# A decoder layer on one core: seven block products for four of 22 pairs of the down product, weight sums made in place, x's scaling and the projections' evictions ahead in VectorE's order

## The chip, the cores and the metric

The kernel runs on one core of a Trainium2 chip. The metric is the device time of one execution, in microseconds (us), as the median of several runs. TensorE (PE in the profile) does the matrix products, VectorE (DVE) and ScalarE (ACT) the elementwise work, GpSimd (POOL) a few fills, and SyncE (SP) issues nearly all DMAs.

## The reference, cut to what matters

```python
def swiglu(x, w_gate, w_up, w_down):
    return (jax.nn.silu(x @ w_gate) * (x @ w_up)) @ w_down
...
h = h + 0.5 * swiglu(rms_norm(h, ffn1_norm), w_gate1, w_up1, w_down1)
p = rms_norm(h, mix_norm) @ w_in
y = concatenate([rwkv7_time_mix(p[..., :3360]), rglru_mix(p[..., 3360:])])
h = h + y @ w_out
h = h + 0.5 * swiglu(rms_norm(h, ffn2_norm), w_gate2, w_up2, w_down2)
return rms_norm(h, final_norm)
```

There are 256 tokens, a model width of 2048, a hidden width of 5632 (44 tiles of 128), and everything is float32.

## The kernel before, in words

**Products.** A float32 product is made of three float32r products: every operand is split into hi (a copy rounded to float32r, made by ScalarE) and lo (the operand less hi, made by VectorE), and `three` (L133 to L138) issues hi times hi, hi times lo and lo times hi into one PSUM bank of 512 columns. So each block of 128 rows of the contraction, 128 tokens and 512 columns costs three matmuls.

**Weights.** They come from memory in pieces of 1 MB (two tiles of 128 rows, 1024 columns) into the buffers `wst` of a pool with three buffers. ScalarE writes `whi` and VectorE writes `wlo`, in pieces of 128x1024, also with three buffers each. `weights` (L49 to L90) does this for the first chunk of gate and up, for the mixer's projections, for the output projection and for all of the down products; the splits are on L81 and L82. `pairs` (L103 to L130) does it for the other chunks of gate and up, by `split` (L93 to L101), whose splits are on L99 and L100.

**Block products.** In those chunks two tiles of 128 rows, the two halves of the tokens and two blocks of 512 columns form a 2 by 2 by 2 product of blocks. A pair of kind "n" takes the plain eight block products (24 matmuls). A pair of kind "S" takes seven (21 matmuls): it needs four sums of weight blocks, made by VectorE into a second buffer of the `wst` pool (L125, L127 and L128), four sums of x's blocks (`sums`), and four more banks (`aux`) for the products that several results share; `shared` adds those together. An S pair splits seven blocks of 128x512 where an n pair splits four. The plans are "nSnSnSnn" for gate and for up, so three of eight pairs are S. A chunk is 1024 columns of the hidden width; the first chunk is 512 wide and takes the plain path.

**Order.** The framework writes out one fixed order for each engine before the run: it walks the program by an estimate of the times and at each point takes, among the instructions that are ready, the one with the smallest number; the number is the place in the program less an offset where `high_priority(offset=...)` stands. The DMAs and splits of weights have an offset of 4000; all else around the change has none.

**x's scaling.** The first chunk multiplies x before the row's norm is known. After each two tiles of the first up product, `normalised` (L274 to L292) scales that pair of x in place, splits it again (ScalarE L281, VectorE L279, L280 and L282), and for the three S pairs makes x's sums (L286 to L289, L291 and L292). The next chunk's gate product needs them.

**Down.** `ffn` ends with the down product: 44 tiles of the hidden values against 1024 columns at a time (in the second feed-forward block 1024, 512 and 512), by `weights` and `rows_times` (L174, L175 and L177). The last chunk's hidden values are transposed (`hidden_T`, 16 transposes on L263, splits on L270 and L271) after 12 of the 44 tiles of the first piece. Each piece ends with four additions of half of a bank to h (L371).

**Mixer.** Each projection (L186 to L188) fills one or two of three banks; its result leaves them on VectorE, multiplied with the row norms (L571 in `shifted`, L895 in `lru`, L935 in `lru_gate`).

Of the kernel before, what the change touches and what calls it, by code (L numbers as in the profile page):

```python
# [18 lines left out]
EPS = 1e-6  # L19


class Core:
# [80 lines left out]
    def pairs(self, mat, c0, plan):  # L103


        nc = self.nc
        ns = plan.count("S")
        ids = {"S": iter(range(ns)), "n": iter(range(ns, self.NK // 2))}
# [31 lines left out]
    def rows_times_pairs(self, mat, c0, plan, own, aux, xhi, xlo, sums, hooks):  # L140
# [3 lines left out]
        for at, (kind, p, w) in enumerate(self.pairs(mat, c0, plan)):  # L144
            first, last = at == 0, at == len(plan) - 1
            if kind == "n":
                for kk in range(2):
                    for t in range(2):
                        x = [v[:, 2 * p + kk, t * P : (t + 1) * P] for v in (xhi, xlo)]
                        for n in range(2):  # L150
                            self.three(own[2 * t + n], x, w[kk][n], first and kk == 0, last and kk == 1)
            else:
                x = lambda k, t: tuple(v[:, 2 * p + k, t * P : (t + 1) * P] for v in (xhi, xlo))
                sm = lambda n: tuple(sums[:, p, h, n * P : (n + 1) * P] for h in range(2))
# [91 lines left out]
def ffn(core, xhi, xlo, rstd, wg, wu, wd, after_first, after_down, fpool, down, rest, back, head=None):  # L246
# [11 lines left out]
    def hidden_T(c0, w, hid):  # L258
        for j in range(0, w // P, 2):
# [13 lines left out]
            )  # L273

    def normalised(p):
# [7 lines left out]
        if p < NSUM:  # L283
            blk = lambda k, t: tmp[:, k, t * P : (t + 1) * P]
            raw = scrap[:, 1, 512:].rearrange("p (n s) -> p n s", n=4)
            nc.vector.tensor_tensor(raw[:, 0], blk(0, 1), blk(1, 1), ALU.add)  # L286
            nc.vector.tensor_tensor(raw[:, 1], raw[:, 0], blk(0, 0), ALU.subtract)
            nc.vector.tensor_tensor(raw[:, 2], blk(0, 0), blk(0, 1), ALU.subtract)
            nc.vector.tensor_tensor(raw[:, 3], blk(1, 0), raw[:, 1], ALU.subtract)  # L289
            flat = raw.rearrange("p n s -> p (n s)")  # L290
            nc.scalar.copy(sums[:, p, 0, :], flat)  # L291
            nc.vector.tensor_tensor(sums[:, p, 1, :], flat, sums[:, p, 0, :].bitcast(F32), ALU.subtract)  # L292
# [12 lines left out]

    pending = []
    ks = list(range(NK))
    for c0, w in chunks:
        if c0:
# [5 lines left out]
            core.rows_times_pairs(wg, c0, GATE_PLAN, own, aux, xhi, xlo, sums, hooks)  # L315
# [5 lines left out]
            core.rows_times_pairs(wu, c0, UP_PLAN, own, aux, xhi, xlo, sums,  # L321
# [4 lines left out]
            pending = [lambda c0=c0, w=w, hid=hid: hidden_T(c0, w, hid)]  # L326
# [15 lines left out]
        for i, (k, hi, lo) in enumerate(core.weights([(wu, c0, w)], ks)):  # L342
# [3 lines left out]
            if i % 2:  # L346
                normalised(i // 2)
# [8 lines left out]
    back()  # L356
    bank0 = 0
    for piece, (c0, w) in enumerate(down):
        nb = w // 512
        db = [[core.bank((bank0 + t * nb + n) % 8) for n in range(nb)] for t in range(NT)]  # L360
        bank0 += NT * nb
        for i, (k, hi, lo) in enumerate(core.weights([(wd, c0, w)], list(range(NF)))):
            core.rows_times(db, hT_hi, hT_lo, k, hi, lo, w, i == 0, i == NF - 1)
            if i == NF // 4:
                for f in pending:
                    f()
                pending = []
# [13 lines left out]
class Mix:  # L381
# [182 lines left out]
    def shifted(self, bks, ntile, mu0, dst):  # L564

        nc = self.nc
        for b, bk in enumerate(bks):
# [321 lines left out]
    def lru(self, hf, bks):  # L889
# [4 lines left out]
        for b, bk in enumerate(bks):  # L894
            nc.vector.tensor_tensor(  # L895
                XB[:, 2 * b : 2 * b + 2, 3:259], bk.rearrange("p (a s) -> p a s", a=2), self.core.rb[:, None, :].to_broadcast([P, 2, 256]), ALU.mult
            )
# [33 lines left out]
    def lru_gate(self, hf, bks, H):  # L931
        nc = self.nc
        G = self.slot("gate")[:, :1024]
        for b, bk in enumerate(bks):
            nc.vector.tensor_tensor(  # L935
                G[:, b * 512 : b * 512 + 512].rearrange("p (a s) -> p a s", a=2),
                bk.rearrange("p (a s) -> p a s", a=2), self.core.rb[:, None, :].to_broadcast([P, 2, 256]), ALU.mult,
            )
# [106 lines left out]
HIDDEN_AT = 6  # L1045


@with_exitstack
def kernel(ctx: ExitStack, tc: tile.TileContext, dram: dict, out: bass.AP):
# [33 lines left out]
    def xt_pool(stack, name, **kw):  # L1083
        pool = stack.enter_context(tc.tile_pool(name=name, bufs=1, **kw))
        return [pool.tile([P, NK, S], F32R, name=name + n) for n in ("hi", "lo")]

    with ExitStack() as front:
        xa = xt_pool(front, "xa")
        with ExitStack() as st:
# [22 lines left out]
            def rest():  # L1112
                return hpool.tile([P, NSUM, 2, 512], F32R, name="xsums1", tag="h")
# [7 lines left out]
            def park(hf):  # L1121
                norm_half(1, hf, *xa)
# [5 lines left out]
                first_norm, park, fpool, [(0, HD), (HD, HD)], rest, back, head={q: partial(norm_quarter, q + 1) for q in range(3)})  # L1128
# [11 lines left out]
        xb = xt_pool(ctx, "xb", **right)  # L1140
# [6 lines left out]
    with ExitStack() as st:  # L1147
# [17 lines left out]
        def rest2():  # L1165
            t = h2.tile([P, core.NT * D + 504], F32R, name="xsums2", tag="h")
            return t[:, : NSUM * 1024].rearrange("p (n h f) -> p n h f", n=NSUM, h=2)
# [3 lines left out]
            lambda: norm_rows(2, 7), closing, fpool, down, rest2, back2)  # L1171
# [37 lines left out]
```

## Time and profile before

| what | value |
|---|---|
| runs | 1953.81, 1951.44, 1953.48 us; median 1953.48 us |
| the profiled execution's own time | 1948.99 us |
| its span | 1947.3 us |
| mean granted clock of TensorE | 0.994 |
| HBM | 184 GB/s over the span |

The profile is of one execution on the chip. A matmul's listed duration overlaps with that of the next, so the pace of a stream is read from the starts. VectorE's instructions overlap a little too. In brackets behind an instruction stands how long its engine idled before it, and what ended that.

### The profile page before, as it was taken

What the parts mean: (1) busy time and instruction counts of PE and PEld (TensorE: products, weight loads), DVE (VectorE), ACT (ScalarE), POOL (GpSimd) and SP (SyncE); (2) the same over time, 40 slices, a digit from 0 to 9 for tenths busy, and PEclk for the clock granted to TensorE, in tenths of its full rate; (3) what the DMA queues carried; (4) which work ended last, traced back from release to release, by engine and by line L of the source; (5) the groups of instructions that cost most, each with busy time, mean ns of one, the idle gap of its engine ahead of it and who ended that gap; (6) DMA issues with size and microseconds to landing.
All of it is one profiled execution on the core that took longest, in us unless ns stands there. A gap on an engine that the chain in (4) does not pass through costs nothing.

```text
span 1947.3 us, 25669 instructions
## 1 busy us (share of the span) xinstructions
PE 1907.3 (98%) x10233; PEld 1589.7 (82%) x10233; DVE 1440.3 (74%) x1822; ACT 985.8 (51%) x1189; POOL 9.9 (1%) x53
## 2 busy tenths in 40 slices
PE   8899999999999999999999999999999999999997
PEld 6678877878888889998899878778888888788886
DVE  5989898888645446876696775899898989844553
ACT  6465555555444335544454555565556555543443
POOL 0000000000000001000000000000000000000000
PEclk9999999999999999999999999999999999999999
DMA  6356555565755556545243456555555655766553
GB/s 238 129 198 214 173 194 195 178 212 190 264 186 204 194 195 207 177 127 163 77 144 115 131 195 215 173 194 182 199 197 198 211 183 184 257 211 193 195 194 129
DMA packets 130032, 360.77 MB, mean 185 GB/s; under 512 B 20879, under 2 KB 23128, under 8 KB 129784
## 3 DMA queue, kind: packets, MB, share of 16 engines
q1 hardware_dynamic: 129592, 358.08, 55.6%
q8 instruction: 80, 1.31, 0.3%
q10 hardware_dynamic: 320, 1.06, 0.1%
q14 instruction: 40, 0.33, 0.0%
HBM read 351.25 MB, written 7.86 MB: 184 GB/s over the span
## 4 chain that ended last, share of the span: by engine, by line
PE 89%; DVE 5%; ACT 3%; issue 2%; DMA 1%; SPq 0%; ACTq 0%; DVEq 0%
PE bank L137 14%; PE bank L136 13%; PE bank L138 13%; PE bank L175 10%; PE bank L177 10%; PE bank L174 10%; PE bank L186 4%; PE bank L188 4%; PE bank L187 4%; ACT whi L99 1%; DVE wlo L82 1%; PE bank L263 1%; DVE wlo L100 1%; PE bank L712 1%; PE bank L640 1%
## 5 line engine op out<-in xcount | busy, mean ns | idle before, releaser
L82 DVE TENSOR_TENSOR wlo<-wst,whi 128x1024 fp32r<-128x1024 f32 (+2 forms) x329 | 398.2, 1212 | 344.6 <-ACT whi L81 343.9
L99 ACT CAST whi<-wst 128x1024 fp32r<-128x1024 f32 (+1 forms) x440 | 430.4, 993 | 364.0 <-PE bank L138 321.9
L81 ACT CAST whi<-wst 128x1024 fp32r<-128x1024 f32 (+2 forms) x329 | 343.2, 1044 | 472.5 <-PE bank L177 335.8
L100 DVE TENSOR_TENSOR wlo<-wst,whi 128x1024 fp32r<-128x1024 f32 (+1 forms) x440 | 493.3, 1147 | 90.9 <-ACT whi L99 85.0
L174 PE MATMUL bank<-whi,hThi 128*128 128x512 f32 x704 | 274.2, 389 | 0.0
L175 PE MATMUL bank<-wlo,hThi 128*128 128x512 f32 x704 | 274.0, 389 | 0.0
L177 PE MATMUL bank<-whi,hTlo 128*128 128x512 f32 x704 | 231.4, 389 | 0.0
L186 PE MATMUL bank<-xahi,whi 128*128 128x256 f32 x688 | 199.1, 290 | 3.2 <-DVE raw L571 3.2
L188 PE MATMUL bank<-xahi,wlo 128*128 128x256 f32 x688 | 197.9, 288 | 0.0
L136 PE MATMUL bank<-whi,xahi 128*128 128x512 f32 x490 | 191.4, 393 | 6.3 <-ACT xahi L281 4.6
L187 PE MATMUL bank<-xalo,whi 128*128 128x256 f32 x688 | 197.3, 287 | 0.0
L137 PE MATMUL bank<-wlo,xahi 128*128 128x512 f32 x490 | 191.5, 391 | 0.6 <-DVE wlo L100 0.6
L136 PE MATMUL bank<-whi,xbhi 128*128 128x512 f32 x490 | 190.2, 391 | 1.9 <-DVE hid L351 1.4
L137 PE MATMUL bank<-wlo,xbhi 128*128 128x512 f32 x490 | 191.1, 390 | 0.6 <-DVE wlo L100 0.6
L138 PE MATMUL bank<-whi,xalo 128*128 128x512 f32 x490 | 191.4, 391 | 0.0
L138 PE MATMUL bank<-whi,xblo 128*128 128x512 f32 x490 | 190.7, 389 | 0.0
L175 PEld LDWEIGHTS bank<-wlo,hThi 128*128 128x128 f32 x704 | 132.2, 188 | 27.4
L177 PEld LDWEIGHTS bank<-whi,hTlo 128*128 128x128 f32 x704 | 132.1, 188 | 27.4
L174 PEld LDWEIGHTS bank<-whi,hThi 128*128 128x128 f32 x704 | 132.2, 188 | 27.1
L186 PEld LDWEIGHTS bank<-xahi,whi 128*128 128x128 f32 x688 | 133.1, 193 | 7.3 <-DVE raw L571 3.6
L188 PEld LDWEIGHTS bank<-xahi,wlo 128*128 128x128 f32 x688 | 132.9, 193 | 1.9 <-issue 1.1
L187 PEld LDWEIGHTS bank<-xalo,whi 128*128 128x128 f32 x688 | 133.1, 194 | 1.2 <-issue 0.2
(298 smaller groups left out, 2557.3 us busy)
## 6 DMA issues: line engine op xcount, KB each, us to landing
wst<-in_ffn_w_up_dram SPq DMA_DIRECT2D x88, 1024.0 KB, 5.0
wst<-in_ffn_w_down_dram SPq DMA_DIRECT2D x88, 1024.0 KB, 4.9
wst<-in_ffn_w_gate_dram SPq DMA_DIRECT2D x87, 1024.0 KB, 5.0
wst<-in_w_in_dram SPq DMA_DIRECT2D x40, 1024.0 KB, 5.0
wst<-in_w_out_dram SPq DMA_DIRECT2D x16, 1024.0 KB, 5.7
h<-parked SPq DMA_DIRECT2D x4, 1024.0 KB, 9.2
wst<-in_w_in_dram SPq DMA_DIRECT2D x4, 640.0 KB, 4.4
h<-in_x_dram SPq DMA_DIRECT2D x4, 512.0 KB, 4.7
```

The costliest lines, as they stand in the source:

```text
L82: nc.vector.tensor_tensor(lo[:, : m * width], src, hi[:, : m * width].bitcast(F32), ALU.subtract)
L99: self.nc.scalar.copy(hv, src)
L100: self.nc.vector.tensor_tensor(lv, src, hv.bitcast(F32), ALU.subtract)
L136: nc.tensor.matmul(out, a[0], b[0], start=first, stop=False)
L137: nc.tensor.matmul(out, a[0], b[1], start=False, stop=False)
L138: self.last_mm = nc.tensor.matmul(out, a[1], b[0], start=False, stop=last)
L174: nc.tensor.matmul(banks[t][n][:, :w], a, whi[:, c : c + w], start=first, stop=False)
L175: nc.tensor.matmul(banks[t][n][:, :w], a, wlo[:, c : c + w], start=False, stop=False)
L177: self.last_mm = nc.tensor.matmul(banks[t][n][:, :w], b, whi[:, c : c + w], start=False, stop=last)
L186: nc.tensor.matmul(out, a, xhi[:, k, :], start=first, stop=False, skip_group_check=True)
L187: nc.tensor.matmul(out, a, xlo[:, k, :], start=False, stop=False, skip_group_check=True)
L188: nc.tensor.matmul(out, b, xhi[:, k, :], start=False, stop=last, skip_group_check=True)
```

## The change

Four things are done.

- The down products of 1024 columns go through `pairs` too. The last four of the 22 pairs (18 to 21, all in the last chunk of the hidden width) are S pairs, at places set by `DOWN_PLAN`. `hidden_T` runs after three pairs and also makes the sums of the hidden blocks, into the second half of x's pool, which is cut in halves for that (`Halves`). `shared_h` adds the shared products to h.
- In `pairs` the four sums of weight blocks are made in place, in the weights' own buffer, after the splits of b11, b21 and b22; the second buffer is gone.
- `normalised` has an offset of 4500.
- The projections' evictions (L571, L895 and L935 before) have an offset of 3900.

```diff
                     b11, b21 = self.split(b[:, :, 0, :], 2)
                     (b22,) = self.split(b[:, 1, 1:2, :], 1)
-                    tt = self.wpool.tile([P, 2 * self.WMAX], F32, name=self.name("wst"), tag="wst")
-                    t = tt.rearrange("p (n f) -> p n f", f=512)
-                    nc.vector.tensor_tensor(t[:, 0:2], b[:, :, 1, :], b[:, 0], ALU.subtract)
-                    t1, t3 = self.split(t[:, 0:2], 2)
-                    nc.vector.tensor_tensor(t[:, 2], t[:, 1], b[:, 0, 0, :], ALU.add)
-                    nc.vector.tensor_tensor(t[:, 3], b[:, 1, 0, :], t[:, 2], ALU.subtract)
-                    t2, t4 = self.split(t[:, 2:4], 2)
+                    w11, w12, w21, w22 = b[:, 0, 0, :], b[:, 0, 1, :], b[:, 1, 0, :], b[:, 1, 1, :]
+                    nc.vector.tensor_tensor(w22, w22, w12, ALU.subtract)
+                    nc.vector.tensor_tensor(w12, w12, w11, ALU.subtract)
+                    nc.vector.tensor_tensor(w11, w22, w11, ALU.add)
+                    nc.vector.tensor_tensor(w21, w21, w11, ALU.subtract)
+                    t1, t3 = self.split(b[:, :, 1, :], 2)
+                    t2, t4 = self.split(b[:, :, 0, :], 2)
...
-    def hidden_T(c0, w, hid):
+    def hidden_T(c0, w, hid, sums=None):
...
+            if sums:
+                if j % 4 == 0:
+                    raw = fpool.tile([P, 4, 512], F32, name=core.name("hsum"), tag="sg")
+                full, r = raw[:, j % 4], raw[:, j % 4 + 1]
+                nc.scalar.copy(full, bk)
+                block_sums(r.rearrange("p (n s) -> p n s", n=4), lambda k, t: full[:, k * 256 + t * P : k * 256 + (t + 1) * P])
+                hi, lo = sums(k // 2)
+                nc.scalar.copy(hi, r)
+                nc.vector.tensor_tensor(lo, r, hi.bitcast(F32), ALU.subtract)
...
+    def shared_h(aux, tmp, c0):
+
+        t1, t2, t3, _ = blocks_of(tmp)
+        nc.scalar.copy(t1, aux[0])
+        nc.vector.tensor_tensor(t2, aux[2], t1, ALU.add)
+        nc.vector.tensor_tensor(t3, aux[3], t2, ALU.add)
+        for (t, n), parts in (((0, 1), (aux[1], t2)), ((1, 0), (t3,)), ((1, 1), (aux[1], t3)), ((0, 0), (t1,))):
+            hs = core.h[:, t, c0 + n * 512 : c0 + (n + 1) * 512]
+            for part in parts:
+                nc.vector.scalar_tensor_tensor(hs, part, 0.5, hs, ALU.mult, ALU.add)
...
             if i % 2:
-                normalised(i // 2)
+                with core.tc.high_priority(offset=4500):
+                    normalised(i // 2)
...
+    hsums = spare()
+    first_s = NF // 2 - 4
+    ids = dict(n=range(first_s), S=range(first_s, NF // 2))
...
+        if w == 1024:
+            own, aux = ([core.bank((bank0 + i) % 8) for i in b] for b in (range(4), range(4, 8)))
+            bank0 += 4
+            plan = DOWN_PLAN[piece]
+            hooks = {}
+            if pending:
+                hooks[DOWN_HIDDEN_AT] = [partial(f, sums=hsums) for f in pending]
+            pending = []
+            tmp = lambda: fpool.tile([P, NT, 1024], F32, name=core.name("dsh"), tag="hid")
+            hooks[plan.rindex("S")] = [lambda: shared_h(aux, tmp(), c0)]
+            core.rows_times_pairs(wd, c0, plan, ids, own, aux, hT_hi, hT_lo, hsums, hooks)
+            db = [own[0:2], own[2:4]]
...
-            nc.vector.tensor_tensor(
-                raw[:, :n, 1:257], bk[:, : n * 256].rearrange("p (a s) -> p a s", a=n), self.core.rb[:, None, :].to_broadcast([P, n, 256]), ALU.mult
-            )
+            with self.tc.high_priority(offset=3900):
+                nc.vector.tensor_tensor(
+                    raw[:, :n, 1:257], bk[:, : n * 256].rearrange("p (a s) -> p a s", a=n),
+                    self.core.rb[:, None, :].to_broadcast([P, n, 256]), ALU.mult,
+                )
...
+DOWN_PLAN, DOWN_HIDDEN_AT = ("nnnnnnSnnnSnnnSnnnSnnn", "nnnSnnnnSnnnnSnnnnSnnn"), 2
```

## Rows read from the trace of the kernel before

**Rows 1.** The page's first part: span, then busy time of each engine.
```profile
span 1947.3 us, 25669 instructions
PE 1907.3 (98%) x10233; PEld 1589.7 (82%) x10233; DVE 1440.3 (74%) x1822; ACT 985.8 (51%) x1189; POOL 9.9 (1%) x53
```

**Rows 2.** The page's fourth part: the chain that ended last, by engine.
```profile
PE 89%; DVE 5%; ACT 3%; issue 2%; DMA 1%; SPq 0%; ACTq 0%; DVEq 0%
```

**Rows 3.** Windows: length, busy us of PE, PEld, DVE, ACT, POOL; granted clock, DMA.
```profile
45.00:70.00 25.00, 18.18 (x77) 14.20 (x76) 23.88 (x40) 13.51 (x17) 0.00 (x0) 0.91 0.39 127
...
120.00:206.00 86.00, 85.93 (x381) 69.13 (x380) 76.83 (x86) 47.27 (x54) 0.00 (x0) 1.00 0.59 195
...
1236.00:1258.00 22.00, 22.00 (x100) 18.28 (x99) 20.93 (x36) 13.13 (x17) 0.00 (x0) 1.00 0.46 144
1258.00:1270.00 12.00, 9.52 (x38) 6.52 (x36) 10.47 (x16) 5.11 (x7) 0.00 (x0) 1.00 0.41 125
...
504.00:753.00 249.00, 249.00 (x1144) 207.24 (x1143) 125.90 (x128) 105.39 (x117) 5.68 (x25) 1.00 0.58 199
```

**Rows 4.** Timeline of PE in a down product: start, duration, instruction.
```profile
1850.10 0.39 PE L174 MATMUL bank<-whi,hThi 128*128 128x512 f32 x1
...
1852.82 0.39 PE L174 MATMUL bank<-whi,hThi 128*128 128x512 f32 x1
```

**Rows 5.** Timeline of PE in two S pairs of the up product.
```profile
129.80 0.39 PE L136 MATMUL bank<-whi,xahi 128*128 128x512 f32 x1
...
132.93 0.40 PE L137 MATMUL bank<-wlo,xsums 128*128 128x512 f32 x1
...
161.63 0.39 PE L136 MATMUL bank<-whi,xahi 128*128 128x512 f32 x1
...
166.71 0.39 PE L137 MATMUL bank<-wlo,xahi 128*128 128x512 f32 x1
```

**Rows 6.** Timeline of ACT in the first of these S pairs.
```profile
130.00 1.05 ACT L99 CAST whi<-wst 128x1024 fp32r<-128x1024 f32 x1 [2.10 <-PE bank L138]
```

**Rows 7.** Timeline of DVE in the same S pair.
```profile
127.63 0.68 DVE L127 TENSOR_TENSOR wst<-wst,wst 128x512 f32<-128x512 f32 x1
128.23 0.68 DVE L100 TENSOR_TENSOR wlo<-wst,whi 128x512 fp32r<-128x512 f32 x1
128.83 0.68 DVE L128 TENSOR_TENSOR wst<-wst,wst 128x512 f32<-128x512 f32 x1
131.08 1.22 DVE L100 TENSOR_TENSOR wlo<-wst,whi 128x1024 fp32r<-128x1024 f32 x1 [1.57 <-ACT whi L99]
```

**Rows 8.** Timeline of PE where the second chunk begins, first feed-forward block.
```profile
60.96 0.39 PE L177 MATMUL bank<-whi,xalo 128*128 128x512 f32 x1
...
69.38 0.80 PE L136 MATMUL bank<-whi,xahi 128*128 128x512 f32 x1 [4.56 <-ACT xahi L281]
...
71.67 0.63 PE L138 MATMUL bank<-whi,xalo 128*128 128x512 f32 x1
72.10 0.48 PE L136 MATMUL bank<-whi,xahi 128*128 128x512 f32 x1
```

**Rows 9.** Timeline of PE at the same place of the second feed-forward block.
```profile
1258.25 0.39 PE L177 MATMUL bank<-whi,xblo 128*128 128x512 f32 x1
...
1262.90 0.40 PE L136 MATMUL bank<-whi,xbhi 128*128 128x512 f32 x1
```

**Rows 10.** Timeline of PE where a projection waits for its bank.
```profile
883.30 0.28 PE L188 MATMUL bank<-xahi,wlo 128*128 128x256 f32 x1
886.62 0.39 PE L186 MATMUL bank<-xahi,whi 128*128 128x256 f32 x1 [3.05 <-DVE raw L571]
```

**Rows 11.** Timeline of DVE at that wait.
```profile
883.56 0.20 DVE L758 TENSOR_TENSOR inv<-inv,invw 64x30 f32<-64x30 f32 x1
...
884.75 1.21 DVE L82 TENSOR_TENSOR wlo<-wst,whi 128x1024 fp32r<-128x1024 f32 x1
885.89 1.27 DVE L571 TENSOR_TENSOR raw<-bank,rb 128x512 f32<-128x512 f32 x2
```

More of the change, by code (lines that the diff above doesn't have):

```diff
@@ L19, with __init__, __getitem__ @@
 EPS = 1e-6
+class Halves:
+    def __init__(self, *tiles):
+        self.tiles = list(tiles)
+    def __getitem__(self, at):
+        rows, k, cols = at
+        if isinstance(k, slice):
+            i, k = k.start // 8, slice(k.start % 8, k.start % 8 + k.stop - k.start)
+        else:
+            i, k = k // 8, k % 8
+        return self.tiles[i][rows, k, cols]
 class Core:
@@ L101, in split, with pairs @@
         return [(hi[:, i * 512 : i * 512 + 512], lo[:, i * 512 : i * 512 + 512]) for i in range(n)]
-    def pairs(self, mat, c0, plan):
+    def pairs(self, mat, c0, plan, ids):
         nc = self.nc
-        ns = plan.count("S")
-        ids = {"S": iter(range(ns)), "n": iter(range(ns, self.NK // 2))}
+        ids = {kind: iter(ps) for kind, ps in ids.items()}
         for kind in plan:
@@ L138, in three, with rows_times_pairs @@
         self.last_mm = nc.tensor.matmul(out, a[1], b[0], start=False, stop=last)
-    def rows_times_pairs(self, mat, c0, plan, own, aux, xhi, xlo, sums, hooks):
+    def rows_times_pairs(self, mat, c0, plan, ids, own, aux, xhi, xlo, sums, hooks):
         ns, done = plan.count("S"), 0
-        for at, (kind, p, w) in enumerate(self.pairs(mat, c0, plan)):
+        for at, (kind, p, w) in enumerate(self.pairs(mat, c0, plan, ids)):
             first, last = at == 0, at == len(plan) - 1
@@ L153, in rows_times_pairs @@
                 x = lambda k, t: tuple(v[:, 2 * p + k, t * P : (t + 1) * P] for v in (xhi, xlo))
-                sm = lambda n: tuple(sums[:, p, h, n * P : (n + 1) * P] for h in range(2))
+                sm = lambda n: tuple(v[:, n * P : (n + 1) * P] for v in sums(p))
                 f, l = done == 0, done == ns - 1
@@ L314, in ffn @@
             hooks.setdefault(HIDDEN_AT, []).extend(pending)
-            core.rows_times_pairs(wg, c0, GATE_PLAN, own, aux, xhi, xlo, sums, hooks)
+            core.rows_times_pairs(wg, c0, GATE_PLAN, ids, own, aux, xhi, xlo, sums, hooks)
             for d, bk in zip(blocks_of(sg), own):
@@ L359, in ffn @@
         nb = w // 512
[L360 to L367, printed above, removed]
+        if w == 1024:
[10 more added lines that the diff above has]
+            db = [own[0:2], own[2:4]]
+        else:
+            db = [[core.bank((bank0 + t * nb + n) % 8) for n in range(nb)] for t in range(NT)]
+            bank0 += NT * nb
+            for i, (k, hi, lo) in enumerate(core.weights([(wd, c0, w)], list(range(NF)))):
+                core.rows_times(db, hT_hi, hT_lo, k, hi, lo, w, i == 0, i == NF - 1)
         for t in range(NT):
@@ L934, in lru_gate @@
         for b, bk in enumerate(bks):
[L935 to L938, printed above, removed]
+            with self.tc.high_priority(offset=3900):
+                nc.vector.tensor_tensor(
+                    G[:, b * 512 : b * 512 + 512].rearrange("p (a s) -> p a s", a=2),
+                    bk.rearrange("p (a s) -> p a s", a=2), self.core.rb[:, None, :].to_broadcast([P, 2, 256]), ALU.mult,
+                )
         nc.scalar.activation(G, G, AF.Gelu_apprx_tanh)
@@ L1084, in xt_pool, with half, sums @@
         pool = stack.enter_context(tc.tile_pool(name=name, bufs=1, **kw))
-        return [pool.tile([P, NK, S], F32R, name=name + n) for n in ("hi", "lo")]
+        def half(n, i):
+            return pool.tile([P, NK // 2, S], F32R, name=core.name(name + n), tag=f"{n}{i}")
+        def sums():
+            tiles = [pool.tile([P, 4, 512], F32R, name=core.name(name + "sum"), tag=f"{n}1") for n in ("hi", "lo")]
+            return lambda p: tuple(t[:, p % 4, :] for t in tiles)
+        return [Halves(half(n, 0), half(n, 1)) for n in ("hi", "lo")], half, sums
     with ExitStack() as front:
-        xa = xt_pool(front, "xa")
+        xa, xa_half, xa_sums = xt_pool(front, "xa")
         with ExitStack() as st:
@@ L1127 @@
             ffn(core, *xa, rstd[0], dram["ffn1_w_gate"][0], dram["ffn1_w_up"][0], dram["ffn1_w_down"][0],
-                first_norm, park, fpool, [(0, HD), (HD, HD)], rest, back, head={q: partial(norm_quarter, q + 1) for q in range(3)})
+                first_norm, park, fpool, [(0, HD), (HD, HD)], rest, back, xa_sums, head={q: partial(norm_quarter, q + 1) for q in range(3)})
         mix_layer(core, dram, *xa, scratch, NSLOT)
```

42 lines of the change are left out of this document (26 added, 16 removed).

## The prediction

> **What bounds the kernel now.** I read the page from the top. PE is busy 1907.3 of 1947.3 us [rows 1] and holds 89% of the chain that ended last [rows 2]; DVE and ACT are the next shares of that chain, 5% and 3%. So a matmul that goes away is time, and anything else counts only where PE waits for it. Next I cut the span into stretches [rows 3]. In the down product (504 to 753 us) PE is busy all the time and DVE for 125.90 of 249 us: nothing holds PE there, and DVE has room. In a middle chunk of gate and up (120 to 206 us) PE is busy 85.93 of 86 us and DVE already 76.83: nearly full. Where the second chunk begins (45 to 70 us) PE is busy only 18.18 of 25 us while DVE works 23.88: there DVE is the bound. The second feed-forward block shows the same in small from 1236 to 1270 us.
>
> Then the starts of single instructions. In a down product twelve matmuls start from 1850.10 to 1852.82 [rows 4]: 2.72 / 12 = 0.2267 us each, the price of a matmul in every sum here. Around 61 to 72 us ten intervals take 11.14 us where 2.27 are due [rows 8]: 8.9 us lost. The largest wait, 4.56 us, ends with x's scaling on ACT (L281). The last rows also show starts 0.43 us apart (71.67 to 72.10), as are the four before them: right after that idle time PE ran at 1.2 GHz, not 2.4, for five matmuls, 1.0 us of the 8.9, and the granted clock of the stretch is 0.91 [rows 3]. At 1258 us six intervals take 4.65 where 1.36 are due [rows 9]: 3.3 us lost. In the mixer one projection waits 886.62 - 883.30 - 0.12 = 3.2 us for its bank, until DVE's eviction L571 [rows 10]; DVE ran the weights' split L82 first [rows 11].
>
> **The change, part by part.** *Block products in down.* There are two pieces of 1024 columns in the first block and one in the second, each with four S pairs: 12 pairs, three matmuls fewer each, 36 x 0.2267 = 8.2 us off. All of it is on the path, since PE never waits there. The Trainium skill, TensorE: Matmul & The Clock Gate, section Back-to-back issue gap, gives a sustained spacing of about 131 ns for 512 columns; by that the 36 matmuls would be worth 4.7 us. The measured 0.2267 us in this very stream decides, and it disagrees.
>
> An S pair asks for four pieces of `whi` and `wlo` where three buffers exist. The third split can start only once PE has left the pair before. In the S pair at 129.80 us ACT's copy starts at 130.00 [rows 6], DVE's lo at 131.08 with 1.22 us [rows 7], and PE is due at the block's hi times lo at about 132.07. The thirteen intervals to 132.93 take 3.13 us where 2.95 are due: 0.18 lost [rows 5]. The S pair at 161.63 us, behind evictions, takes 5.08 us for 21 intervals where 4.76 are due: 0.32 lost. The new S pairs meet the same three buffers, with DVE half idle, so I take 0.18: 12 x 0.18 = 2.2 us back on; bounds 0 and 12 x 0.32 = 3.8.
>
> *What goes beside it.* `hidden_T` runs after three pairs instead of after six. Its 16 transposes on PE are the same; new are, for each of four banks, two ACT passes and two groups on DVE (four sums of 128 columns, one lo of 512), some 1.5 us by the 0.60 us of a 512 wide pass, so 6 us of DVE. The first S pair of the first piece is three plain pairs later, 3 x 24 x 0.2267 = 16 us, of which DVE needs 3 x 2 x 1.22 = 7 for splits [rows 7]. `shared_h` is one ACT copy and eight DVE passes of about 0.6 us, 5 us, with three pairs behind it before its banks are wanted. Each S pair adds one and a half splits of 1024 and four sums, 1.5 x 1.22 + 4 x 0.60 = 4.2 us of DVE, and 1.6 of ACT; eight pairs make 34 us against 123 idle in the first block's down [rows 3]. I cost all this at nothing; if that cover were gone, the 5 us of `shared_h` would stand in front of the next piece, three times. No DMA is added; the second `wst` buffer that an S pair gives up can only let SP issue sooner, and PE waits for no load here.
>
> *Sums in place.* In the 60 S pairs of gate and up, one pass of 1024 and two of 512 become four of 512. Starts of 512 wide passes lie 0.60 us apart [rows 7], so DVE's work is the same to 0.1 us. The order is not: the first sums wrote another buffer and could run any time after the load; now they overwrite the blocks, so they follow b22's lo. In the rows: b22's lo is at 128.23, done at about 128.83; two sums end at 130.03; the copy of t1 and t3 starts at 130.00 today because its buffer came then. There is no slack left, and none lost: DVE idles 1.57 us there today. Bounds: -1 (the three early passes no longer push other work) and 60 x 0.32 = 19 (below, a rival). I take +0.5.
>
> *x's scaling ahead.* Now the scaling goes before the splits. Both are DVE's and both are needed: the splits by the up product that runs, the scaling by the gate product after it. From 45 to 70 us DVE idled 1.1 of 25 us, from 1236 to 1270 us 2.6 of 34 [rows 3]. Changing the order of a full engine makes no room; what can come off is part of its idle time and the slow clock, if the one long wait is cut into short ones. What is late next: the splits of the up product, then the first S pair's sums, behind the scaling of pairs not needed yet. I take -1.5 in the first block and -0.5 in the second. Bounds: all of 8.9 and 3.3 off; or worse than today by a scaling with x's sums (four passes of 0.60 and four small ones, some 3.2 us, plus a split of 1.22 against 12 x 0.2267 = 2.72 us of PE: 1.7 late for each of three pairs, 5.0, less the one pair, 2.7 us, that the splits are ahead), +2.3 each.
>
> *Evictions ahead.* At 883.56 us DVE ends a small product of the inversion; L571 then comes only at 885.89 [rows 11]. With its offset it is ready at 883.4 and may start at 883.8, the first of the two is done some 0.65 us later, and PE goes on at about 884.5: -2.1. POOL's fill of the row's first column keeps its place; it writes another column, and the eviction needs no wait for it. Bounds: -3.2, and +1.2 if the split L82 that is pushed back is what PE misses next. The other evictions held nothing up.
>
> Sum: -8.2 + 2.2 + 0.5 - 1.5 - 0.5 - 2.1 = -9.6. The profiled execution took 1948.99 us, 4.5 below the median of 1953.48, with 1.7 around its span. So 1939.4 for an execution like that one, and 1953.48 - 9.6 = 1943.9, 1944.0 for the median. About 0.2%, 3.9 us, is what a measurement of this kernel can tell from no change.
>
> **Rivals.** *The new order clears the waits.* If splits slip into the gaps between dependent scaling passes, PE loses next to nothing at 61 and 1258 us: 8.9 + 3.3 off instead of 2.0, so 1944 - 10.2 = 1933.8. For it: the wait's named end is x's scaling. Against: DVE's 23.88 of 25. Chance 0.15.
>
> *The scaling starves the up product.* The upper bounds hold: 2 x 2.3 in place of -2.0, so 1944 + 6.6 = 1950.5, about no change. For it: DVE is full there and the up product's splits now stand behind. Against: dependent passes leave places that a ready split can take. Chance 0.18.
>
> *Late sums slow every S pair.* In place sums put two DVE passes between b22's lo and the copy of t1 and t3, with no slack in the rows. If other DVE work of half a pass gets in between, each of 60 S pairs loses 0.32 us more: +19.2 - 0.5, so 1944 + 18.7 = 1962.7, slower. It decides from 10.1 / 60 = 0.17 us per pair on. For it: DVE is busy 76.83 of 86 us in a chunk. Against: the evictions that now stand in the way would use the time in which the early sums ran. Chance 0.11.
>
> *The removed matmuls are worth less.* If 131 ns were their worth, 3.5 us less: 1947.4. That is the skill page's figure; no stream in this trace shows it. Chance 0.02.
>
> **How the numbers follow.** The forecast has 0.54; its own range, from the bounds of the small terms, is 1939 to 1949.5. Range: 1934 to 1952.5 takes in it, the starving case and half of the clearing case; left out are the other half and the slower rival, 0.19. Faster by over 0.2% (under 1949.6): 0.54 of the forecast nearly whole (0.49), 0.15, 0.06 of the starving case and 0.02: 0.72. Within 0.2%: 0.05 and 0.12, 0.17. Slower: 0.11.
>
> **What would show it.** Right: PE has 36 matmuls fewer; in the down products its starts stay 0.2267 us apart but for about 0.2 us in each S pair; 60 to 75 us and 1258 to 1263 us still cost PE most of what they do, with DVE full; the 3.2 us at 883 us shrink to about one; the middle chunks keep their 86.5 us. Wrong: a middle chunk longer by over 1 us (late sums), waits of PE for `wlo` in the first up product (starving), or no wait left at the second chunk's begin (clearing).

## The result, and the profile after

The changed kernel takes 1986.45 us (median of four runs, 1983.61 to 1986.71), where the kernel before takes 1952.46 us beside it: a ratio of 1.0172, with a 95% interval of 1.0154 to 1.0189. I had forecast 1944.0 us and a gain.

The page of the kernel after, span, busy times and chain (compare [rows 1, 2]):

```profile
span 1985.0 us, 25861 instructions
...
PE 1918.5 (97%) x10197; PEld 1591.2 (80%) x10197; DVE 1547.3 (78%) x2018; ACT 1015.1 (51%) x1232; POOL 9.7 (0%) x53
...
PE 70%; DVE 21%; ACT 6%; issue 2%; DMA 0%; ACTq 0%; SPq 0%; DVEq 0%
...
L151 PE MATMUL bank<-whi,xsums 128*128 128x512 f32 x240 | 89.9, 415 | 21.2 <-ACT whi L114 21.2
```

The same group of matmuls in the list of the kernel before:

```profile
L136 PE MATMUL bank<-whi,xsums 128*128 128x512 f32 x240 | 86.2, 400 | 1.3 <-ACT whi L99 0.6
```

The 36 matmuls are gone (10233 to 10197), and the chain has moved: PE has lost 19 points of it and DVE has gained 16. Ahead of the matmuls of the S pairs with x's sums (L151, L136 before) PE now idles 21.2 us for ACT, where it idled 1.3 us before.

Windows of the kernel after, columns as in [rows 3]: a middle chunk and the first down product.

```profile
120.00:206.00 86.00, 83.22 (x365) 66.11 (x364) 76.01 (x87) 45.41 (x52) 0.00 (x0) 1.00 0.56 195
524.30:766.80 242.50, 240.17 (x1068) 196.42 (x1067) 170.18 (x197) 117.01 (x131) 0.46 (x5) 1.00 0.58 198
```

The middle chunk is where it went. In 86 us PE starts 365 matmuls instead of 381, with the same granted clock of 1.00 and no more DVE work (76.01 us against 76.83). From one chunk's transposes to the next chunk's it is some 86.6 us before and 90.4 after, 3.8 us more. Ten chunks make 38 us; the two spans are 37.7 us apart. Both gate and up stretches show it (from the first S pair of a block to its down product): 426.2 to 446.3 us and 426.1 to 445.9. The down products hardly changed: 243.1 to 242.5 and 252.6 to 252.6 us.

The reason shows in one S pair of that chunk, the up product's second. In such a pair b11, b21 and b22 are blocks of the weights and t1 to t4 their four sums: the first two passes make t3 and t1, the last two t2 and t4, and each of the seven blocks is split into hi and lo. The chain of waits around it, kernel after (start, us, what):

```profile
132.50 0.63 ACT whi L114
...
133.16 0.70 DVE wlo L115
...
133.89 0.70 DVE wst L139
...
134.61 0.70 DVE wst L140
...
135.34 0.70 DVE wst L141
...
136.07 0.70 DVE wst L142
...
136.87 1.06 ACT whi L114
...
137.97 0.50 PE bank L151
```

It reads from top to bottom: b22's hi on ACT, its lo on DVE, the four sums one after the other, then the hi of t2 and t4 on ACT, and only then the matmul. Each step starts where the one above it ends. The timelines of ACT and PE in the same pair show what hangs on it:

```profile
135.42 1.05 ACT L114 CAST whi<-wst 128x1024 fp32r<-128x1024 f32 x1 [2.29 <-DVE wst L140]
136.87 2.00 ACT L114 CAST whi<-wst 128x1024 fp32r<-128x1024 f32 x2 [0.40 <-DVE wst L142]
...
136.16 0.39 PE L153 MATMUL bank<-whi,xalo 128*128 128x512 f32 x1
...
137.06 0.62 PE L151 MATMUL bank<-whi,xsums 128*128 128x512 f32 x2
137.97 0.50 PE L151 MATMUL bank<-whi,xsums 128*128 128x512 f32 x1 [0.29 <-ACT whi L114]
...
139.93 0.39 PE L152 MATMUL bank<-wlo,xahi 128*128 128x512 f32 x1
```

From 136.16 to 139.93 lie 14 intervals, 3.77 us where 14 x 0.2267 = 3.17 are due: 0.60 lost, against 0.18 in [rows 5]. Four of a chunk's six S pairs lose 0.6 us like this, and the gate product's third, which has the transposes beside it, loses 0.2. The gate product's first is worse, because the evictions of the up product before it (L365, L366) come in between the passes. (The pair at 161.63 us in [rows 5] is that same place in the kernel before: it belongs to the next chunk's gate product, not to the up product.) DVE's timeline, kernel after:

```profile
165.63 0.69 DVE L115 TENSOR_TENSOR wlo<-wst,whi 128x512 fp32r<-128x512 f32 x1
166.24 0.69 DVE L366 TENSOR_TENSOR hid<-hid,sg 128x512 f32<-128x512 f32 x1
166.84 0.68 DVE L139 TENSOR_TENSOR wst<-wst 128x512 f32<-128x512 f32 x1
167.45 0.69 DVE L365 TENSOR_TENSOR hid<-bank,hid 128x512 f32<-128x512 f32 x1
168.05 0.68 DVE L140 TENSOR_TENSOR wst<-wst 128x512 f32<-128x512 f32 x1
168.65 0.69 DVE L366 TENSOR_TENSOR hid<-hid,sg 128x512 f32<-128x512 f32 x1
169.25 0.68 DVE L141 TENSOR_TENSOR wst<-wst 128x512 f32<-128x512 f32 x1
169.92 1.23 DVE L115 TENSOR_TENSOR wlo<-wst,whi 128x1024 fp32r<-128x1024 f32 x1
171.06 0.68 DVE L142 TENSOR_TENSOR wst<-wst 128x512 f32<-128x512 f32 x1
```

From b22's lo to the last sum it is 171.06 - 165.63 = 5.4 us here instead of 2.9, and by PE's starts (168.86 to 174.95 us, 15 intervals, 6.09 us where 3.40 are due) this pair loses 2.7 us. Together 4 x 0.6 + 0.2 + 2.7 = 5.3 us a chunk. By the same count the kernel before loses 1.7; the difference, 3.6, is near the 3.8 us by which a chunk has grown.

### The profile page after: what moved, and what is told of

It is laid out like the page before. It is cut to its first block, busy times and chain, and to the rows that moved or that the text cites. A ratio compares the mean times of both kernels' runs of the same rounds, so it can differ in the third digit from the quotient of the medians.

```text
span 1985.0 us, 25861 instructions
## 1 busy us (share of the span) xinstructions
PE 1918.5 (97%) x10197; PEld 1591.2 (80%) x10197; DVE 1547.3 (78%) x2018; ACT 1015.1 (51%) x1232; POOL 9.7 (0%) x53
## 4 chain that ended last, share of the span: by engine, by line
PE 70%; DVE 21%; ACT 6%; issue 2%; DMA 0%; ACTq 0%; SPq 0%; DVEq 0%
PE bank L152 14%; PE bank L153 14%; PE bank L151 13%; DVE wlo L115 6%; ACT whi L114 5%; PE bank L190 4%; PE bank L192 4%; PE bank L189 4%; PE bank L201 4%; PE bank L202 4%; PE bank L203 4%; DVE wst L140 2%; DVE wst L141 2%; DVE wst L139 2%; DVE wst L142 2%
## 5 line engine op out<-in xcount | busy, mean ns | idle before, releaser
L114 ACT CAST whi<-wst 128x1024 fp32r<-128x1024 f32 x596 | 588.7, 1001 | 593.0 <-PE bank L153 365.1
L115 DVE TENSOR_TENSOR wlo<-wst,whi 128x1024 fp32r<-128x1024 f32 x596 | 678.4, 1158 | 175.9 <-ACT whi L114 171.3
L97 DVE TENSOR_TENSOR wlo<-wst,whi 128x1024 fp32r<-128x1024 f32 (+2 forms) x197 | 236.7, 1204 | 164.2 <-ACT whi L96 162.0
L96 ACT CAST whi<-wst 128x1024 fp32r<-128x1024 f32 (+2 forms) x197 | 204.1, 1037 | 262.6 <-PE bank L192 122.9
L151 PE MATMUL bank<-whi,xahi 128*128 128x512 f32 x490 | 190.3, 395 | 3.0 <-ACT whi L114 2.1
L151 PE MATMUL bank<-whi,xbhi 128*128 128x512 f32 x490 | 188.6, 392 | 0.9 <-ACT whi L114 0.9
L153 PE MATMUL bank<-whi,hTlo 128*128 128x512 f32 x468 | 182.4, 390 | 0.0
L152 PE MATMUL bank<-wlo,hThi 128*128 128x512 f32 x468 | 182.3, 390 | 0.0
L151 PE MATMUL bank<-whi,hThi 128*128 128x512 f32 x468 | 181.8, 391 | 0.0
L151 PEld LDWEIGHTS bank<-whi,xahi 128*128 128x128 f32 x490 | 92.8, 190 | 24.6 <-ACT whi L114 4.2
L151 PE MATMUL bank<-whi,xsums 128*128 128x512 f32 x240 | 89.9, 415 | 21.2 <-ACT whi L114 21.2
L152 PEld LDWEIGHTS bank<-wlo,xahi 128*128 128x128 f32 x490 | 92.7, 189 | 20.6 <-DVE wlo L115 1.4
```

Of the source, the lines that this page charges most:

```text
L96: self.last_split = nc.scalar.copy(hi[:, : m * width], src)
L97: nc.vector.tensor_tensor(lo[:, : m * width], src, hi[:, : m * width].bitcast(F32), ALU.subtract)
L114: self.nc.scalar.copy(hv, src)
L115: self.nc.vector.tensor_tensor(lv, src, hv.bitcast(F32), ALU.subtract)
L151: nc.tensor.matmul(out, a[0], b[0], start=first, stop=False)
L152: nc.tensor.matmul(out, a[0], b[1], start=False, stop=False)
```

## The experiments

**One part at a time.** *Changed kernel, sums back in a second buffer*:

```diff
-                    nc.vector.tensor_tensor(w22, w22, w12, ALU.subtract)
...
+                    tt = self.wpool.tile([P, 2 * self.WMAX], F32, name=self.name("wst"), tag="wst")
...
+                    nc.vector.tensor_tensor(t[:, 0:2], b[:, :, 1, :], b[:, 0], ALU.subtract)
```

> The changed kernel, with the four sums of weight blocks made in the second buffer as before the change (one pass of 1024, two of 512, free to run before the splits); the other three parts stay. Theory A (the sums in place are the loss: PE's lost time per chunk of gate and up went from 1.7 to 5.6 us, all of it in the S pairs): the ten chunks go back by 3.8 us each and the twelve S pairs of down lose 0.2 us each instead of 0.45, so the span falls from 1985.0 by 38 + 3 to about 1944, some 4 below the kernel before; a chunk takes 86.6 us again. Theory B (the new places of x's scaling and of the evictions push the splits of all chunks back): the chunks stay near 90.4 us and the span stays above 1975. Theory C (the four new S pairs per piece of down, with their extra DVE work, are the loss): it stays above 1975 too, with down as long as in the changed kernel.

Measured: 1947.4 us, ratio to the kernel before 0.998 (0.9972 to 0.9988), and most chunks take 86.7 us again. The first theory holds.

*Kernel before, sums in place, nothing else*:

```diff
-                    nc.vector.tensor_tensor(t[:, 0:2], b[:, :, 1, :], b[:, 0], ALU.subtract)
...
+                    nc.vector.tensor_tensor(w22, w22, w12, ALU.subtract)
+                    nc.vector.tensor_tensor(w12, w12, w11, ALU.subtract)
+                    nc.vector.tensor_tensor(w11, w22, w11, ALU.add)
+                    nc.vector.tensor_tensor(w21, w21, w11, ALU.subtract)
```

> The kernel before, with only the sums of weight blocks made in place. Theory A: the ten chunks grow by 3.8 us each, 1947 + 38 = 1985 us span; down, mixer and the first chunk stay. Theory B or C: within 3 us of the kernel before.

Measured: 1986.59 us against 1951.79, ratio 1.0174 (1.0159 to 1.0188), and 90.33 us a chunk. In place sums alone cost 34.8 us by the medians; by the stretches of gate and up in this run's trace (445.6 and 445.4 us against 426.2 and 426.1) it is 38.8. No run explains the four us between these counts; the medians are used below. Taking the sums out of the changed kernel gives 1986.45 - 1947.4 = 39.1 back. The difference to 34.8 fits the down products, which have S pairs there: in the changed kernel they take 242.5 and 252.6 us, with the second buffer 239.9 and 251.0, so 4.2 us less. This part is the whole loss.

*Kernel before, block products in down, nothing else* (the first of the four parts):

```diff
+            core.rows_times_pairs(wd, c0, plan, ids, own, aux, hT_hi, hT_lo, hsums, hooks)
...
+DOWN_PLAN, DOWN_HIDDEN_AT = ("nnnnnnSnnnSnnnSnnnSnnn", "nnnSnnnnSnnnnSnnnnSnnn"), 2
```

> The kernel before, with only the block products in the three 1024 wide pieces of down (sums of weight blocks in the second buffer, x's scaling and evictions where they were). Theory A: 36 matmuls less, 8.2 us, and 0.18 to 0.3 us lost in each of twelve S pairs, 2.2 to 3.8 us: 4.4 to 6.0 us below the kernel before, chunks at 86.6 us. Theory C: slower than the kernel before.

Measured: 1947.32 us, ratio 0.9976 (0.9967 to 0.9984), so -4.5 us. The down products take 239.9 and 251.0 us instead of 243.1 and 252.6: -3.2 and -1.6. The windows of the first one in this run and in the kernel before, one line each:

```profile
504.60:744.40 239.80, 239.80 (x1065) 195.78 (x1064) 167.40 (x189) 117.02 (x130) 0.00 (x0) 1.00 0.57 201
```
```profile
503.20:746.20 243.00, 243.00 (x1089) 201.17 (x1087) 119.96 (x113) 99.47 (x104) 0.00 (x0) 1.00 0.58 197
```

PE is busy throughout with 24 matmuls fewer and DVE does 47 us more beside it: the cover I named was there. Of 24 x 0.2267 = 5.44 us, 2.2 are lost again in eight S pairs, 0.28 each.

*Kernel before, x's scaling ahead, nothing else*:

```diff
-                normalised(i // 2)
+                with core.tc.high_priority(offset=4500):
+                    normalised(i // 2)
```

> The kernel before with x's scaling ahead and nothing else. My prediction gave it -2.0 us (-1.5 in the first block, -0.5 in the second), its rivals -12 (clears the waits) and +4.6 (starves the up product). From the run with the sums back in a second buffer I now expect nothing: the long wait before the second chunk gets about 4 us shorter in each block and the first S pair of the up product then loses some 2.7 us, and what is left drowns. So 1951 to 1952 us where the kernel before has 1951.8 to 1952.5, a ratio of 0.999 to 1.0005. If the scaling were what made the changed kernel slow: above 1960 us.

Measured: 1950.89 us, ratio 0.9995 (0.9986 to 1.0004). PE in the gate product's second S pair, second chunk of this run (not of the up product, as the expectation has it):

```profile
85.47 0.39 PE L136 MATMUL bank<-whi,xsums 128*128 128x512 f32 x1
...
87.02 0.74 PE L136 MATMUL bank<-whi,xsums 128*128 128x512 f32 x2 [0.71 <-ACT whi L99]
88.28 0.51 PE L137 MATMUL bank<-wlo,xsums 128*128 128x512 f32 x1 [0.52 <-DVE wlo L100]
90.04 0.50 PE L136 MATMUL bank<-whi,xsums 128*128 128x512 f32 x1 [0.56 <-ACT whi L99]
...
91.56 0.39 PE L137 MATMUL bank<-wlo,xsums 128*128 128x512 f32 x1
```

From 85.47 to 91.56 lie 13 intervals, 6.09 us where 2.95 are due: 3.1 lost, where the same pair lost 0.2 in the kernel before. DVE makes this pair's first sums (L125) only at 84.60 us, between two passes that scale an x pair needed only later (L280 at 83.99, L282 at 85.73); in the kernel before it makes them at 81.07.

Ahead of the second chunk PE now loses 7.3 us instead of 8.9 [rows 8]. Its waits have become one, of 4.1 us, but the starts behind it lie 0.43 us or more apart for fourteen intervals, from 64.67 to 71.04 us, instead of six before (69.38 to 72.10). PE ran at 1.2 GHz there; the granted clock of that stretch is 0.50:

```profile
64.60:71.00 6.40, 6.33 (x14) 4.64 (x15) 5.43 (x9) 1.15 (x3) 0.00 (x0) 0.50 0.30 123
```

By the stretches, the first S pair starts 2.3 us earlier in the first block, and from there to the down product it takes 2.0 us longer; in the second block (from the output projection) it is 2.8 earlier and 3.2 longer. From the start to the first down product it is 503.0 us against 503.2. A wash.

*Kernel before, evictions ahead, nothing else* (this at all three places):

```diff
+            with self.tc.high_priority(offset=3900):
+                nc.vector.tensor_tensor(
```

> The kernel before with the offset of 3900 on the projections' evictions and nothing else. My prediction gave it -2.1 us, from a wait of 3.2 us shrinking to about one. In the changed kernel VectorE still runs the copy and the weights' split before the eviction, so I now expect the wait to stay at 3.1 to 3.2 us and the time to be that of the kernel before within 0.1% (1950.5 to 1953). If the evictions do matter elsewhere in the mixer: a stretch from the first projection to the output projection shorter or longer than 368.1 us by over 1 us.

Measured: 1953.84 us, ratio 1.001 (1.0001 to 1.0019). The wait at 883 us stays at 3.2 us [rows 10], and the stretch from the first projection to the output projection takes 373.0 us against 368.1: if anything, slower. (Of all runs here, that stretch took 370.1 to 373.0 us in the five with the offset and 366.9 to 369.9 in those without, but 372.5 in the one with two weight buffers.) The order on DVE in this run answers to [rows 11]:

```profile
883.62 0.20 DVE L759 TENSOR_TENSOR inv<-inv,invw 64x30 f32<-64x30 f32 x1
883.86 1.02 DVE L763 COPY invw<-inv 64x1024 f32<-64x1024 f32 x1
884.80 1.21 DVE L82 TENSOR_TENSOR wlo<-wst,whi 128x1024 fp32r<-128x1024 f32 x1
885.93 1.27 DVE L572 TENSOR_TENSOR raw<-bank,rb 128x512 f32<-128x512 f32 x2
```

The copy and the split still run before the eviction; the offset has changed nothing there.

**What costs in the in place sums.** They differ from the old ones in two ways: they are four passes in a row, each of which reads what an earlier one wrote or overwrites what it reads, and they overwrite what the splits must read first. *Changed kernel, the same four passes into a second buffer* keeps the four passes and drops the overwriting. (Of the dependences, the third pass keeps that on the first and the fourth that on the third; the second no longer depends on the first.)

```diff
-                    nc.vector.tensor_tensor(w22, w22, w12, ALU.subtract)
-                    nc.vector.tensor_tensor(w12, w12, w11, ALU.subtract)
...
+                    nc.vector.tensor_tensor(t[:, 1, 1, :], w22, w12, ALU.subtract)
+                    nc.vector.tensor_tensor(t[:, 0, 1, :], w12, w11, ALU.subtract)
```

> The changed kernel with the same four passes in the same order, each dependent on the one before as there, but written into a second weights' buffer, so that they need not wait for the splits of b11, b21 and b22. If the loss comes from overwriting (the passes can start only after b22's lo, and t1's and t3's split behind them), the loss goes: about 1947 to 1950 us, 86.7 to 87.4 us a chunk. If it comes from four dependent passes 0.73 us apart in place of three 0.60 apart, it stays: about 1980 to 1986 us, 90 us a chunk.

Measured: 1946.85 us, ratio 0.9973 (0.9962 to 0.9983), and 86.5 us a chunk. Its DVE in one S pair:

```profile
124.58 0.68 DVE L141 TENSOR_TENSOR wst<-wst 128x512 f32<-128x512 f32 x1
125.18 2.35 DVE L115 TENSOR_TENSOR wlo<-wst,whi 128x1024 fp32r<-128x1024 f32 x2
127.45 0.68 DVE L142 TENSOR_TENSOR wst<-wst 128x512 f32<-128x512 f32 x1
128.30 0.69 DVE L115 TENSOR_TENSOR wlo<-wst,whi 128x512 fp32r<-128x512 f32 x1 [0.17 <-ACT whi L114]
128.91 0.69 DVE L143 TENSOR_TENSOR wst<-wst,wst 128x512 f32<-128x512 f32 x1
129.63 0.69 DVE L144 TENSOR_TENSOR wst<-wst,wst 128x512 f32<-128x512 f32 x1
```

Two of the four passes now run before b22's lo, between the splits, and two after it; 128.91 to 129.63 is the same 0.72 us between dependent passes as in the slow kernel. So it is the overwriting that costs: it puts all four passes behind b22's lo.

*Changed kernel, b22 split first, sums in place* lets the first two passes, which overwrite only w22 and w12, start before b11's and b21's splits:

```diff
-                    b11, b21 = self.split(b[:, :, 0, :], 2)
                     (b22,) = self.split(b[:, 1, 1:2, :], 1)
+                    b11, b21 = self.split(b[:, :, 0, :], 2)
```

> The changed kernel with one line moved: in an S pair b22 is split before b11 and b21. The sums stay in place, four passes. Theory A1 (what costs time is that the sums must follow b22's split, and that this split gets its buffer only when PE is half through the pair before): b22's split now takes the buffer that comes free one split earlier, the two sums that t1 and t3 need are done before their buffer is free, and the chunks return to within 1 us of 86.6 us: span 1943 to 1953. Theory A2 (four dependent passes, 0.73 us apart, are too much for DVE wherever they stand): the chunks stay above 89 us, span above 1972.

Measured: 1954.09 us, ratio 1.0012 (1.0004 to 1.0021), and 87.4 us a chunk. Theory A1 holds: most of the loss goes, with the sums still in place and four passes. What is left against the second buffer, 0.7 us a chunk, is in one pair: the gate product's first, behind the evictions, loses 1.1 us, the other five about 0.2 to 0.3 each, as in the kernel before.

*The same without offsets, with four buffers for each split and two for the weights*:

```diff
-                st = self.wpool.tile([P, 2 * self.WMAX], F32, name=self.name("wst"), tag="wst")
+                st = self.wpool.tile([P, 2 * self.WMAX], F32, name=self.name("wst"), tag="wst", bufs=2)
...
-        hi = self.wpool.tile([P, self.WMAX], F32R, name=self.name("whi"), tag="whi")
+        hi = self.wpool.tile([P, self.WMAX], F32R, name=self.name("whi"), tag="whi", bufs=4)
```

> A version that could beat both: block products in down and sums in place, with b22 split first, no offsets, two buffers of the weights in place of three and four of each split in place of three (the same memory). If PE's waits in S pairs come from the three split buffers, an S pair's four splits now fit and the 1.7 us that a chunk of the kernel before loses mostly go, ten times, and some 0.3 us in each of twelve S pairs of down: 1930 to 1936 us, a chunk near 85.2 us. If the loads become the bound, since only one can now be ahead of the splits (5.0 us from issue to landing against 5.4 us of PE in a plain pair), PE waits for wst at most pairs: above 1960 us.

Measured: 2066.95 us, ratio 1.0588 (1.0574 to 1.0603). From its list of waits (us in total, times, longest):

```profile
ACT whi L114 <- DMA wst<-in_ffn_w_gate_dram: 156.8, 44, 5.1
ACT whi L114 <- DMA wst<-in_ffn_w_up_dram: 132.7, 33, 4.7
```

The rival came true: the splits wait for loads. The first down product, where three plain pairs stand between two S pairs, still takes 239.9 us, while a chunk takes some 98. That fits an S pair holding its buffer through the sums and so making the next load late; no run takes that apart.

**Versions without the parts that do not pay.** *The run with four passes in a second buffer, less the evictions' offset* (this at all three places):

```diff
-            with self.tc.high_priority(offset=3900):
+            with self.tc.high_priority(offset=0):
```

> The run with the four passes in a second buffer, less the offset on the projections' evictions; block products in down and x's scaling ahead stay. In the runs so far the stretch from the first projection to the output projection took 370.1 to 373.0 us with the offset and 368.1 to 369.9 without. If that is the offset's doing, the stretch falls to about 368.5 here and the time by 1 to 2 us below the 1946.9 of that run: 1944 to 1946 us. If the offset does nothing: 1946 to 1948 us.

Measured: 1944.49 us, ratio 0.9963 (0.9951 to 0.9976); the stretch falls from 370.1 to 368.1 us, as the first theory had it, though the intervals of the two runs overlap.

*The same, less the scaling's offset too*:

```diff
-                with core.tc.high_priority(offset=4500):
+                with core.tc.high_priority(offset=0):
```

> The same, less the offset of x's scaling too: block products in down and the four passes in a second buffer, nothing else. If the scaling ahead gives back in the first S pair of the up product what it takes off before the second chunk, the sum of the stretches around both (start to the down product, output projection to the second down product) is the same as with it to 2 us and the time is that of the run with it within 0.1%. If it gains the 2.0 us that I predicted, this is slower than that run by 2 us. If the four passes are better than the three of the kernel before by themselves, this lies below 1947.3, the time of the block products in down alone.

Measured: 1942.07 us, ratio 0.995 (0.9936 to 0.9964), the lowest median of all, and faster than both kernels. It is not slower than the run with the scaling ahead, so in this kernel the scaling ahead does not gain the 2.0 us that I predicted; the two intervals overlap, so a gain without it is not shown either. A middle chunk of this run has all its matmuls back:

```profile
120.00:206.00 86.00, 85.92 (x381) 69.18 (x380) 76.65 (x92) 47.67 (x54) 0.00 (x0) 1.00 0.58 195
```

*Kernel before, the four passes in a second buffer, nothing else*:

```diff
-                    nc.vector.tensor_tensor(t[:, 0:2], b[:, :, 1, :], b[:, 0], ALU.subtract)
...
+                    nc.vector.tensor_tensor(t[:, 1, 1, :], w22, w12, ALU.subtract)
+                    nc.vector.tensor_tensor(t[:, 0, 1, :], w12, w11, ALU.subtract)
```

> The kernel before with the four passes written into the second buffer and nothing else. The run with these and the block products in down took 1942.1 us (ratio 0.995), that with the block products in down alone 1947.3 (0.9976). If the four passes are worth the 5 us between them, since the first of them no longer waits behind a pass of 1024 and their order lets t1's and t3's split start earlier: 1946 to 1948 us, ratio 0.997 to 0.998. If the 5 us are from how the rest of the order falls out in that one program (the stretch from the output projection to the second block differs by 3.8 us between the two): 1950.5 to 1953 us, a ratio within 0.1% of 1.

Measured: 1950.87 us, ratio 0.9996 (0.9986 to 1.0005). So the passes are worth nothing by themselves, and why the version without offsets lies 5 us below the block products in down alone stays open: the stretches in which those two differ most (157.1 to 153.3 us from the output projection to the second block's first S pair, 368.4 to 366.9 in the projections) hold no S pair.

*The version without offsets, the copy behind the inversion on ACT*:

```diff
-        nc.vector.tensor_copy(XT, X.rearrange("q s t -> q t s"))
+        nc.scalar.copy(XT, X.rearrange("q s t -> q t s"))
```

> The run without offsets, and the copy of 64x1024 that ends the first inversion moved from VectorE to ScalarE (both inversions of the mixer use that line). In the kernel before VectorE runs copy, split and eviction one after the other (1.03, 1.21 and 0.6 us) while TensorE waits 3.2 us for the eviction. If that order on VectorE is what TensorE waits for, the wait falls by the copy's 1.0 us to about 2.2 us. If the copy only stands in time that VectorE would idle, waiting for the split's ScalarE half or for the bank, the wait stays at 3.2 us. The whole time changes by less than can be measured either way; the reading is the wait.

Measured: 1943.15 us, ratio 0.9955 (0.9943 to 0.9968), no difference to the run without it. But the wait answers. DVE, ACT and PE in this run's timeline:

```profile
879.82 0.20 DVE L816 TENSOR_TENSOR inv<-inv,invw 64x30 f32<-64x30 f32 x1
879.94 1.21 DVE L97 TENSOR_TENSOR wlo<-wst,whi 128x1024 fp32r<-128x1024 f32 x1
881.07 1.27 DVE L628 TENSOR_TENSOR raw<-bank,rb 128x512 f32<-128x512 f32 x2
...
880.05 2.00 ACT L820 COPY invw<-inv 64x1024 f32<-64x1024 f32 x1 [2.85 <-DVE inv L816]
...
879.55 0.28 PE L205 MATMUL bank<-xahi,wlo 128*128 128x256 f32 x1
881.80 0.39 PE L203 MATMUL bank<-xahi,whi 128*128 128x256 f32 x1 [1.97 <-DVE raw L628]
```

Counted as for [rows 10], 881.80 - 879.55 - 0.12 = 2.13 us instead of 3.2: what PE waits for there is indeed what stands before the eviction on DVE.

## Why the prediction was wrong

**Sums in place, "I take +0.5": the step that failed.** It cost 34.8 us in gate and up by the medians, and some 4 more in down. I had the right places in view: b22's lo, the sums behind it, the copy of t1 and t3. Three things were wrong in the working.

- I followed the chain to the copy of t1 and t3 alone and counted two passes behind b22's lo. The pair needs t2 and t4 as well, so four passes and a second copy stand there. [rows 7] show it: before, only two sums lie near b22's lo (127.63 and 128.83, the first of them ahead of it), and L125's 1024 wide pass was done two splits earlier (124.22, below). That DVE's work stays the same was true (76.01 us in the chunk against 76.83) and beside the point.
- The passes that depend on each other start 0.72 to 0.73 us apart, not 0.60. That is 0.1 us each, a small part: the run with b22 split first has the same spacing and loses 0.2 to 0.3 us in five of six S pairs.
- "There is no slack left, and none lost" set a term of zero slack at nearly zero. With no slack, each late pass is lost time.

DVE in the kernel before, just ahead of [rows 7]:

```profile
124.22 1.22 DVE L125 TENSOR_TENSOR wst<-wst 128x1024 f32<-128x1024 f32 x1
125.36 2.35 DVE L100 TENSOR_TENSOR wlo<-wst,whi 128x1024 fp32r<-128x1024 f32 x2
```

The rival of late sums had the place, and a chance of 0.11. Its price, 0.32 us a pair, was taken from a pair that waits for evictions in the kernel before. Measured are 34.8 / 60 = 0.58 us more a pair on average. In four of a chunk's six pairs it is 0.3 more, near the rival's price, but without the other DVE work in between that the rival asked for: four passes are enough. In the gate product's first the evictions do come in between, and that pair alone makes over half of the loss (2.7 us against 0.3). I had counted the evictions as harmless there. At 0.58 the rival gives 1944 - 0.5 + 34.8 = 1978 us; most of the rest up to 1986.45 is in the three points below.

**Block products in down: right in kind.** Predicted -8.2 + 2.2 = -6.0, measured -4.5 us by the medians and -4.8 by the stretches. The starts between the S pairs' waits stay at 0.2267 us; the turnaround costs 0.28 us a pair, between my 0.18 and my upper bound of 0.32. In the changed kernel the late sums ate it: 0.6 of 5.4 us are left in the first block, nothing in the second. The starts give the net -3.2 us of the first block as 5.44 off and 2.2 back on. By the Trainium skill's 131 ns a matmul (TensorE: Matmul & The Clock Gate, section Back-to-back issue gap) an estimate for 24 matmuls is 3.1 us. That this comes close is chance: the trace has 226.7 ns between starts.

**x's scaling ahead: -2.0 predicted, -0.9 measured with an interval around zero** (-2.7 to +0.8 us, so that run alone does not exclude the -2.0). The time lost ahead of the second chunk shrank by the 1.5 us that I took, from 8.9 to 7.3, but not as I thought: three waits became one of 4.1 us, and the slow clock lasted longer. What I named as late next, an S pair's sums behind the scaling of pairs not needed yet, gave the gain back, and I had put no price on it. Neither rival came true in full: 8.9 us became 7.3, not nothing and not 11.

**Evictions ahead: -2.1 predicted, +2.1 measured by itself.** The interval of that +2.1 is 0.2 to 3.7 us; it fits the longer stretch of the mixer, and why that grows is open. I took it that an offset moves an instruction in DVE's order. Here the copy and the split kept their places ahead of the eviction. That fits an order written from estimated times, in which an instruction passes only others that are ready at the same estimated moment; for the split, its own larger offset of 4000 would fit as well. No run tells these apart. What DVE runs before the eviction is what PE waits for, as the run with the copy on ACT shows, so the wait was read rightly and the offset did not move it.

By the medians the parts add up to -4.5 + 34.8 + 4.3 - 0.9 + 2.1 = 35.8, measured 34.0 (4.3 being the down products' share of the late sums, 39.1 - 34.8). The 39.1 comes from the changed kernel itself, so this is not a test of its own.

## What to carry to other kernels

An in place update saves a buffer and adds an edge: each write has to wait for every reader of what it overwrites. Before taking it as free, follow the chain from the last of those readers to the last consumer of the new values, count every pass and copy on it, and compare that with the time the consumer leaves; the sum of the work says nothing. A priority offset is a wish: look whether the order has changed before crediting it.

## What was not expected of the hardware

- Passes of 128x512 on DVE of which each reads what the one before wrote, or overwrites what it reads, start 0.72 to 0.73 us apart; independent ones start 0.60 apart, at the same listed 0.68 to 0.69 us. With one independent pass in between, two dependent ones start 1.21 us apart (166.84 to 168.05), so that pass takes 0.48 us of the chain and not 0.60.
- The copy of 64x1024 behind the inversion takes 1.02 us on DVE and 2.00 on ACT.
